# HGRN level operands copied aside for three tiled runs per unit, and a longer hold of whole-array products in the merge of threads

## The chip, the cores and the metric

One NeuronCore of a Trainium2 chip runs one launch of the kernel. The metric is device time in microseconds. The core has five engines with queues of their own: TensorE (PE; its weight loads are listed as PEld), VectorE (DVE), ScalarE (ACT), GpSimd (POOL) and SyncE (SP, which issues most DMAs).

## The reference, cut to what matters

The reference is one inference step of a two-layer trunk: layer 0 is a gated DeltaNet beside sliding-window attention, layer 1 is HGRN2. A prompt of 2048 positions and a sample group of 8 x 8 positions share all weights. After each mixer stands an output part (projection, layer norm, gate). The change touches the HGRN2 recurrence, for each of 8 heads with 128 x 128 state:

```python
fg = lb + (1.0 - lb) * jax.nn.sigmoid(zf)
logf = jnp.log(jnp.maximum(fg, F_FLOOR))
k = (1.0 - lb) * jax.nn.sigmoid(-zf)
...
# S_t = diag(f_t) S_{t-1} + k_t v_t^T,  o_t = S_t^T q_t / sqrt(dk)
dec = masked_exp(causal, G_c[:, :, :, None, :] - G_c[:, :, None, :, :])
a = jnp.einsum('nhid,nhijd,nhjd->nhij', q_c, dec, k_c)
o = jnp.einsum('nhid,nhde->nhie', q_c * jnp.exp(G_c), s) + jnp.einsum('nhij,nhje->nhie', a, v_c)
```

For one pair of positions j < i of a chunk the matrix `a` holds the sum over the 128 channels of q_i, k_j and the product of the decays f between them.

## The kernel before

**Work.** Time runs through four stages: layer 0's mixer, layer 0's output part (`dense_post`), the HGRN mixer (`dense_hgrn`), layer 1's output part. In each, one low-priority thread `dense` issues the big projections as split-precision products, three 128 x 128 matmuls per slice of the contraction (`product`). Its results go to many small threads: attention tiles, DeltaNet units, HGRN units. In the HGRN mixer the loop runs over halves of the prompt, heads and groups of 128-position chunks; each (head, group) is a unit (`hgrn_unit`). The groups have 4, 2, 2, 4 and 4 chunks, so there are 24 units of four chunks and 16 of two; for one group the 64 sample positions follow (`hgrn_sample`, 8 units). At most three units are in flight (`UNITS`), and each reserves memory before it starts: `7 * ... + RH` columns of an arena of 50 x 1024.

**HGRN core.** `hgrn_core` (L1716) builds `A`, the matrix `a` transposed, chunk by chunk, by doubling levels. Operands q and k are scaled in place on DVE so that, at level s, the k of the left half of each block of 2s positions and the q of the right half carry all decays between them. Then the products of that level are matmuls on TensorE with 32 columns of k as weights (`prod`), and their place in the 32 x 32 diagonal block is picked by a mask (`copy_predicated` on DVE). Levels 1 and 2 and the diagonal are made as elementwise products and summed over channels by matmuls with a matrix of ones (`sums`). Levels 32 and 64 go straight into `A` by ACT copies. As q and k are scaled in place, scaling to level 2s waits until TensorE has read level s. So a unit issues six separate runs of small matmuls: `sums`, 4, 8, 16, 32, 64.

**Tiled and whole.** A matmul whose weights have 32 or 64 rows or columns uses a part of the array ("tiled"); several of them run side by side. The rest are 128*128 ("whole"). In the profile the form of a weight load (128*32, 128*64, 32*32) tells which.

**Order of work.** All threads are Python generators; `run` (L525) is a list scheduler at build time that merges them into one fixed order for each engine. It keeps a model clock per engine, ranks the next instruction of each thread by when it could start, and emits the first. A TensorE instruction is ranked `MARGIN` (700 ns) after its operands are ready. The model counts 100 ns for a change from whole to tiled and 213 ns back (`SWITCH`), and these lines keep the rank free of the change itself but put whole products `STAY` later while the array stands tiled:

```python
s = self.start(o, MARGIN if o.eng == "tensor" else 0, True)
if o.eng == "tensor" and self.mode != o.mode:
    s -= SWITCH[o.mode == WHOLE] - STAY * (o.mode == WHOLE)
```

The order is fixed at build time; on the chip every engine works through its queue and waits on semaphores where an operand is late. All instructions are issued by one helper (line L354), so the profile's rows are told apart by tile names: `ar` is the arena, `bank` PSUM, `cst` the constants.

Of the kernel before, what the change touches and what calls it, by code (L numbers as in the profile page):

```python
# [46 lines left out]
FIRSTW, LASTG, WO0, WO1, GB = 30, 12, 6, 8, 2  # L47
PREP, WG0 = 2, 1
DMARGIN = 0
RD, RH = 8, 256  # L50
NBLK = 50
UNITS = (6, 5, 3)
XBUDGET = [18, 20]
# [524 lines left out]
class Step(Sched):  # L578
# [1134 lines left out]
        u["f"], u["k"] = e1, e2  # L1713
        self.dirty = True

    def hgrn_core(self, np_, n, cs, q, k, f, levels, out, own):  # L1716
# [33 lines left out]
        for s in levels + (2 * levels[-1],):  # L1750
            if s > 1:
                hs, nbk = s // 2, W // s
                qv = QF.rearrange("p (b r i) -> p b r i", r=2, i=hs)
                kv = k.rearrange("p (b r i) -> p b r i", r=2, i=hs)
                bv = B.rearrange("p (b r) -> p b r", r=2)
                yield self.V.tensor_tensor(out=qv[:, :, 1, :], in0=qv[:, :, 1, :], in1=bc(bv[:, :, 0], 2, hs), op=ALU.mult)
                yield self.V.tensor_tensor(out=kv[:, :, 0, :], in0=kv[:, :, 0, :], in1=bc(bv[:, :, 1], 2, hs), op=ALU.mult)
                if Bs is None:
                    Bs = yield al(W)
                B = Bs[:, bo : bo + nbk]  # L1760
                bo += nbk
                yield self.V.tensor_tensor(out=B, in0=bv[:, :, 0], in1=bv[:, :, 1], op=ALU.mult)
                if s == 2 and own:
                    self.free(f)
            if s > levels[-1]:
                break
            if s == 1:
                continue
            ps = yield bank()
            if s == 2:  # L1770
                Q4, K4, P4 = cut(QF, 4), cut(k, 4), kdb[:, :W].rearrange("p (b j i) -> p b j i", j=2, i=2)
                for j in range(2):
                    yield self.V.tensor_tensor(out=P4[:, :, j, :], in0=Q4[:, :, 2:4], in1=bc(K4[:, :, j], 2, 2), op=ALU.mult)
                yield from sums(ps, n * 48, Ab, 32)
                yield from sums(ps, 0, P1[:, : W // 2], 16)
                yield from sums(ps, n * 16, kdb[:, :W], 32)
                yield self.V.tensor_tensor(out=Dv, in0=cut(ps[:np_, n * 48 : n * 80], 32), in1=bc(self.c("ident32")[:np_], 1, n), op=ALU.mult)
                yield self.G.memset(ap=Ab[:np_], constant=0.0)
                D2, D4 = Dv.rearrange("p c (b i) -> p c b i", i=2), Dv.rearrange("p c (b i) -> p c b i", i=4)
                yield self.V.copy_predicated(out=D2[:, :, :, 1], mask=bc(cut(self.c("m1")[:np_], 2)[:, :, 1].bitcast(U32), 1, n), data=cut(ps[:np_, : n * 16], 16))  # L1780
                for j in range(2):
                    d = ps[:np_, n * 16 : n * 48].rearrange("p (c b j i) -> p c b j i", b=8, j=2, i=2)[:, :, :, j, :]
                    yield self.V.copy_predicated(out=D4[:, :, :, 2:4], mask=bc(cut(self.c(("m2", "m2o")[j])[:np_], 4)[:, :, 2:4].bitcast(U32), 1, n), data=d)
                self.free(P1)
            elif s <= 16:
                yield from prod(ps, QF)
                yield self.V.copy_predicated(out=Dv, mask=bc(self.c(f"m{s}")[:np_].bitcast(U32), 1, n), data=cut(ps[:np_, : n * 32], 32))
            else:

                cor = [(j, s) for j in range(0, 128, 2 * s)]  # L1790
                for c in range(n):
                    for j, _ in cor:
                        t = c * cs + j
                        yield self.P.matmul(out=ps[j : j + s, c * s : (c + 1) * s], lhsT=k[:, t : t + s], rhs=QF[:, t + s : t + 2 * s], start=True, stop=True)
                for j, _ in cor:
                    yield self.A.activation(out=A[j : j + s, :, j + s : j + 2 * s], in_=cut(ps[j : j + s, : n * s], s), func=AF.Copy)
# [12 lines left out]
    def hgrn_unit(self, half, h, hh, gi, u, vs):  # L1809
# [50 lines left out]
    def hgrn_sample(self, h, q, k, f, v, sg):  # L1860
# [4 lines left out]
        yield from self.hgrn_core(ST, 1, ST, q, k, f, (1, 2, 4), r, False)  # L1865
# [279 lines left out]
```

## Time and profile before

| | us |
|---|---|
| median of 3 runs | 3143.66 |
| lowest, highest | 3141.78, 3158.1 |
| profiled execution, its own time | 3148.57 |
| its span in the trace | 3146.8 |

| slice of the span | PE busy | DVE busy | ACT busy | granted PE clock |
|---|---|---|---|---|
| 0 to 400 us | 371.08 | 258.89 | 206.74 | 0.96 |
| 800 to 1200 us | 382.80 | 283.40 | 221.12 | 0.97 |
| 1200 to 1600 us | 395.36 | 163.98 | 55.43 | 1.00 |
| 2000 to 2400 us | 387.59 | 282.65 | 140.39 | 0.98 |

Each row of the second table is a stretch of 400 us; the columns are the time in which the engine executed something. A PE that is busy is not a PE at its peak: a weight load that cannot overlap, or a pause shorter than the matmul pipeline, hides in it. The profile's own mean for a matmul includes its passage through the array, so the pace is read from the distance between starts.

### The profile page before, as it was taken

To read this page: it belongs to the slowest core of one execution; us is meant where nothing else is said; L and a number is where in the kernel's file an instruction comes from. 1 tells how busy PE (TensorE), PEld (TensorE's weight loads), DVE (VectorE), ACT (ScalarE), POOL (GpSimd) and SP (SyncE) were. 2 spreads that over 40 slices of the span, in tenths; PEclk is the share of its full clock that TensorE was granted. 3 is DMA by queue.
4 is the path that set the end of the run, shared out by engine and by line. 5 is a ranking of instruction groups with operands and counts; after the bars stand their busy time and mean duration, and the time that the engine had idled before them with its cause. 6 is when DMAs were issued, how large, how long until landed. Compare 5 with 4: busy or idle time off the path is not lost.

```text
span 3146.8 us, 63372 instructions
## 1 busy us (share of the span) xinstructions
PE 3054.1 (97%) x25592; PEld 2507.9 (80%) x25592; DVE 1962.1 (62%) x5693; ACT 1149.5 (37%) x3074; POOL 197.1 (6%) x265
## 2 busy tenths in 40 slices
PE   8999899999999999999999999998999999999999
PEld 7787777877877787878888888786888888787787
DVE  5567776776757674333457686868577576733333
ACT  4455454655555561111143332324333333311011
POOL 0000000000000001111000000000000000111110
PEclk9999999999989999999999999999999999999999
DMA  4231222321214264233322122213111121732331
GB/s 118 70 86 41 59 69 61 95 63 47 81 48 121 77 174 107 75 82 89 104 74 69 42 69 67 65 56 99 56 52 52 46 69 49 221 87 75 82 86 49
DMA packets 320837, 246.45 MB, mean 78 GB/s; under 512 B 33800, under 2 KB 285840, under 8 KB 320528
## 3 DMA queue, kind: packets, MB, share of 16 engines
q1 hardware_dynamic: 253408, 207.80, 21.8%
q0 software_dynamic: 67136, 34.61, 6.1%
q8 instruction: 201, 3.29, 0.4%
q14 instruction: 92, 0.75, 0.1%
HBM read 182.98 MB, written 60.45 MB: 77 GB/s over the span
## 4 chain that ended last, share of the span: by engine, by line
PE 57%; DVE 7%; DMA 4%; issue 3%; ACT 2%; POOL 0%; SPq 0%; POOLq 0%; DVEq 0%; ACTq 0%
PE bank L354 57%; DVE ar L354 7%; DMA ar<-in_w_in_odd 2%; ACT ar L354 2%; DMA ar<-in_w_in_even 1%; POOL ar L354 0%; SPq L354 0%; DMA ar<-gd 0%; DMA ar<-in_w_ple_gate 0%; DMA ar<-x 0%; DMA os<-ar 0%; ACT L354 0%; DMA ar<-in_w_out_even 0%; DMA ctail<-ar 0%; DMA gd<-ar 0%
## 5 line engine op out<-in xcount | busy, mean ns | idle before, releaser
L354 PE MATMUL bank<-ar,ar 128*128 128x512 f32 (+10 forms) x20168 | 2865.9, 306 | 55.5 <-DVE ar L354 30.8
L354 PEld LDWEIGHTS bank<-ar,ar 128*128 128x128 f32 (+4 forms) x20168 | 2250.9, 163 | 490.4 <-issue 85.8
L354 ACT ACTIVATE ar<-bank 128x128 f32<-128x128 f32 (+13 forms) x1471 | 528.0, 369 | 1343.8 <-PE bank L354 1250.5
L354 DVE TENSOR_TENSOR ar<-ar,ar 128x256 f32<-128x256 f32 (+9 forms) x1517 | 737.1, 514 | 245.2 <-ACT ar L354 207.5
L354 ACT ACTIVATE ar<-ar 128x1024 fp32r<-128x1024 f32 (+12 forms) x833 | 443.1, 551 | 581.7 <-DMA ar<-in_pT 248.6
L354 DVE SCALAR_TENSOR_TENSOR ar<-ar,bank 128x512 f32<-128x512 f32 (+3 forms) x256 | 164.1, 641 | 393.4 <-ACT ar L354 261.6
L354 PE MATMUL bank<-cst,ar 128*128 128x128 f32 (+4 forms) x1439 | 244.2, 280 | 21.1 <-DVE ar L354 14.7
L354 PEld LDWEIGHTS bank<-cst,ar 128*128 128x128 f32 (+4 forms) x1439 | 172.9, 141 | 72.4 <-issue 19.0
L354 DVE TENSOR_TENSOR ar<-bank,ar 128x128 fp32r<-128x128 f32 (+7 forms) x326 | 147.6, 455 | 80.7 <-ACT ar L354 45.2
L354 POOL TENSOR_TENSOR ar<-ar,mhalf 128x2 f32<-128x2 f32 (+3 forms) x104 | 107.6, 1035 | 1361.6 <-DVE ar L354 978.5
L354 DVE TENSOR_TENSOR ar<-ar 128x256 f32<-128x256 f32 (+11 forms) x575 | 135.6, 248 | 15.4 <-ACT ar L354 14.1
L354 DVE SCALAR_TENSOR_TENSOR ar<-bank,ar,ar 128x509 f32<-128x509 f32 (+8 forms) x216 | 123.0, 573 | 26.2 <-ACT ar L354 24.7
L354 DVE COPY_PREDICATED ar<-cst,bank 128x128 f32<-128x128 uint32 (+4 forms) x356 | 93.0, 262 | 72.7 <-PE bank L354 61.5
L354 PEld LDWEIGHTS bank<-ar 128*32 128x32 f32 (+4 forms) x2904 | 90.5, 121 | 45.5 <-DVE ar L354 17.9
L354 PE MATMUL bank<-ar 128*32 128x32 f32 (+5 forms) x2904 | 116.8, 212 | 8.2 <-DVE ar L354 6.9
L354 DVE SCALAR_TENSOR_TENSOR ar<-ar,ar,bank 128x128 f32<-128x128 f32 x192 | 65.7, 342 | 74.1 <-PE bank L354 72.6
L354 POOL MEMSET ar<- 128x256 f32 (+4 forms) x85 | 29.0, 348 | 1141.7 <-PE bank L354 772.8
L354 DVE SCALAR_TENSOR_TENSOR ar<-ar,ar,ar 128x1024 f32<-128x1024 f32 (+1 forms) x68 | 87.0, 1279 | 13.4 <-POOL ar L354 13.3
L354 POOL DMA_DIRECT2D ar<-os x64 | 57.4, 898 | 283.1 <-PE bank L354 214.1
L354 DVE SCALAR_TENSOR_TENSOR ar<-ar,ar 128x512 f32<-128x512 f32 (+10 forms) x187 | 55.9, 304 | 30.4 <-ACT ar L354 29.1
L354 DVE TENSOR_SCALAR ar<-bank 128x512 f32<-128x512 f32 (+2 forms) x80 | 44.6, 592 | 36.2 <-ACT ar L354 35.8
L354 ACT ACTIVATION_READ_ACCUMULATOR ar<-bank 128x1 f32 (+1 forms) x340 | 66.4, 195 | 0.2
(55 smaller groups left out, 820.7 us busy)
## 6 DMA issues: line engine op xcount, KB each, us to landing
ar<-os POOLq DMA_DIRECT2D x64, 512.0 KB, 4.9
ar<-in_w_in_odd SPq DMA_DIRECT2D x64, 512.0 KB
ar<-in_w_in_even SPq DMA_DIRECT2D x60, 512.0 KB
os<-ar SPq DMA_DIRECT2D x36, 512.0 KB
ar<-x SPq DMA_DIRECT2D x32, 512.0 KB
os<-ar SPq DMA_DIRECT2D x56, 256.0 KB
ar<-in_x_prompt SPq DMA_DIRECT2D x16, 512.0 KB
ar<-in_w_ple_gate SPq DMA_DIRECT2D x16, 512.0 KB
```

What stands on the lines that cost most here:

```text
L354: o.fn = lambda: f(**kw)
```

## The change

`hgrn_core` gets a flag `deep` (true for the prompt, false for the samples) in place of the list of levels. For the prompt, ACT copies the scaled k and the right halves of q of level 4 into `KA`, `QA` and those of level 8 into `KB`, `QB`, so that DVE can go on scaling in place; then levels 4, 8 and 16 are multiplied in one run into one bank, with 16 moved columns in place of 32. In the same way the operands of level 32 are copied to `KC`, `QC`, and levels 32 and 64 share a run and a bank. A unit has three runs. `level` copies 16 columns per chunk where 32 were copied. For the samples, level 4 follows `sums` in the same run. The reserve per unit grows (`RH`), and `STAY` goes from 40 to 1000 ns.

```diff
-RD, RH = 8, 256
+RD, RH = 8, 512
...
-STAY = 40
+STAY = 1000
...
+        def scale(s):
+            nonlocal B, Bs, bo
+            hs, nbk = s // 2, W // s
+            qv = QF.rearrange("p (b r i) -> p b r i", r=2, i=hs)
+            kv = k.rearrange("p (b r i) -> p b r i", r=2, i=hs)
+            bv = B.rearrange("p (b r) -> p b r", r=2)
+            yield self.V.tensor_tensor(out=qv[:, :, 1, :], in0=qv[:, :, 1, :], in1=bc(bv[:, :, 0], 2, hs), op=ALU.mult)
+            yield self.V.tensor_tensor(out=kv[:, :, 0, :], in0=kv[:, :, 0, :], in1=bc(bv[:, :, 1], 2, hs), op=ALU.mult)
...
-        def prod(ps, qq):
+        def prod(ps, c0, kk, qq):
             for c in range(n):
                 for r in range(nb):
-                    t = slice(c * cs + 32 * r, c * cs + 32 * r + 32)
-                    yield self.P.matmul(out=ps[rows[r], c * 32 : c * 32 + 32], lhsT=k[:, t], rhs=qq[:, t], start=True, stop=True)
+                    t = c * cs + 32 * r
+                    yield self.P.matmul(out=ps[rows[r], c0 + c * 16 : c0 + c * 16 + 16], lhsT=kk[:, t : t + 32], rhs=qq(c * nb + r), start=True, stop=True)
...
+        def level(ps, c0, s):
+            d = Dv.rearrange("p c (b r i) -> p c b r i", r=2, i=s)[:, :, :, 1, :]
+            m = self.c(f"m{s}")[:np_].rearrange("p (b r i) -> p b r i", r=2, i=s)[:, :, 1, :]
+            x = ps[:np_, c0 : c0 + n * 16].rearrange("p (c b i) -> p c b i", c=n, i=s)
+            yield self.V.copy_predicated(out=d, mask=bc(m.bitcast(U32), 1, n), data=x)
...
-            elif s <= 16:
-                yield from prod(ps, QF)
-                yield self.V.copy_predicated(out=Dv, mask=bc(self.c(f"m{s}")[:np_].bitcast(U32), 1, n), data=cut(ps[:np_, : n * 32], 32))
...
+            KA, QA = kdb, P1
+            ops = []
+            for s, kk, qq in ((4, KA, QA), (8, KB, QB)):
+                yield self.A.activation(out=kk[:, :W], in_=k, func=AF.Copy)
+                yield self.A.activation(out=cut(qq[:, : W // 2], s), in_=right(QF, s), func=AF.Copy)
+                ops.append((kk, cut(qq[:, : W // 2], 16)))
+                yield from scale(2 * s)
             ps = yield bank()
...
+            for i, (kk, qq) in enumerate(ops):
+                yield from prod(ps, i * n * 16, kk, lambda b: qq[:, b])
+            q16 = right(QF, 16)
+            yield from prod(ps, 2 * n * 16, k, lambda b: q16[:, b])
+            self.free(P1, QB)
+            yield from scale(32)
+            KC, QC = (cut(KB[:, i * W // 2 : (i + 1) * W // 2], 32) for i in range(2))
+            yield self.A.activation(out=KC, in_=k.rearrange("p (b r i) -> p b r i", r=2, i=32)[:, :, 0, :], func=AF.Copy)
+            yield self.A.activation(out=QC, in_=right(QF, 32), func=AF.Copy)
+            for i, s in enumerate((4, 8, 16)):
+                yield from level(ps, i * n * 16, s)
             self.freebank(ps)
+            yield from scale(64)
+            ps = yield bank()
+            for c in range(n):
+                for b in range(2):
+                    yield self.P.matmul(out=ps[64 * b : 64 * b + 32, c * 32 : (c + 1) * 32], lhsT=KC[:, 2 * c + b], rhs=QC[:, 2 * c + b], start=True, stop=True)
+            for c in range(n):
+                t = c * cs
+                yield self.P.matmul(out=ps[0:64, n * 32 + c * 64 : n * 32 + (c + 1) * 64], lhsT=k[:, t : t + 64], rhs=QF[:, t + 64 : t + 128], start=True, stop=True)
...
-        yield from self.hgrn_core(128, nt, 128, q[:, :Wp], k[:, :Wp], f[:, :Wp], SMALL + (32, 64), r, not smp)
+        yield from self.hgrn_core(128, nt, 128, q[:, :Wp], k[:, :Wp], f[:, :Wp], True, r, not smp)
```

More of the change, by code (lines that the diff above doesn't have):

```diff
@@ L1714, in gates, with hgrn_core @@
         self.dirty = True
-    def hgrn_core(self, np_, n, cs, q, k, f, levels, out, own):
+    def hgrn_core(self, np_, n, cs, q, k, f, deep, out, own):
         W = n * cs
@@ L1728, in hgrn_core, with right @@
         B = f
-        def prod(ps, qq):
+        def scale(s):
[6 more added lines that the diff above has]
+            yield self.V.tensor_tensor(out=kv[:, :, 0, :], in0=kv[:, :, 0, :], in1=bc(bv[:, :, 1], 2, hs), op=ALU.mult)
+            if Bs is None:
+                Bs = yield al(W)
+            B = Bs[:, bo : bo + nbk]
+            bo += nbk
+            yield self.V.tensor_tensor(out=B, in0=bv[:, :, 0], in1=bv[:, :, 1], op=ALU.mult)
+        def prod(ps, c0, kk, qq):
             for c in range(n):
                 for r in range(nb):
-                    t = slice(c * cs + 32 * r, c * cs + 32 * r + 32)
-                    yield self.P.matmul(out=ps[rows[r], c * 32 : c * 32 + 32], lhsT=k[:, t], rhs=qq[:, t], start=True, stop=True)
+                    t = c * cs + 32 * r
+                    yield self.P.matmul(out=ps[rows[r], c0 + c * 16 : c0 + c * 16 + 16], lhsT=kk[:, t : t + 32], rhs=qq(c * nb + r), start=True, stop=True)
+        def right(x, s):
+            return x.rearrange("p (b r i) -> p b r i", r=2, i=s)[:, :, 1, :]
+        def level(ps, c0, s):
[3 more added lines that the diff above has]
+            yield self.V.copy_predicated(out=d, mask=bc(m.bitcast(U32), 1, n), data=x)
         def sums(ps, c0, x, w):
@@ L1749, in hgrn_core @@
         yield self.V.tensor_tensor(out=P1[:, : W // 2], in0=Q2[:, :, 1], in1=K2[:, :, 0], op=ALU.mult)
[L1750 to L1768, printed above, removed]
-            ps = yield bank()
[L1770 to L1784, printed above, removed]
-            elif s <= 16:
-                yield from prod(ps, QF)
-                yield self.V.copy_predicated(out=Dv, mask=bc(self.c(f"m{s}")[:np_].bitcast(U32), 1, n), data=cut(ps[:np_, : n * 32], 32))
[L1788 to L1796, printed above, removed]
-            self.freebank(ps)
@@ new lines, in hgrn_core @@
+        yield from scale(2)
+        if own:
+            self.free(f)
+        Q4, K4, P4 = cut(QF, 4), cut(k, 4), kdb[:, :W].rearrange("p (b j i) -> p b j i", j=2, i=2)
+        for j in range(2):
+            yield self.V.tensor_tensor(out=P4[:, :, j, :], in0=Q4[:, :, 2:4], in1=bc(K4[:, :, j], 2, 2), op=ALU.mult)
+        if deep:
+            KB = yield al(W)
+            QB = yield al(W // 2)
+        else:
+            yield from scale(4)
+        ps = yield bank()
+        yield from sums(ps, n * 48, Ab, 32)
@@ new lines, in hgrn_core @@
+        yield from sums(ps, 0, P1[:, : W // 2], 16)
+        yield from sums(ps, n * 16, kdb[:, :W], 32)
+        if deep:
+            yield from scale(4)
+        else:
+            q4 = QF.rearrange("p (g b r i) -> p g b r i", b=4, r=2, i=4)[:, :, :, 1, :]
+            yield from prod(ps, n * 80, k, lambda b: q4[:, b])
+        yield self.V.tensor_tensor(out=Dv, in0=cut(ps[:np_, n * 48 : n * 80], 32), in1=bc(self.c("ident32")[:np_], 1, n), op=ALU.mult)
+        yield self.G.memset(ap=Ab[:np_], constant=0.0)
@@ new lines, in hgrn_core @@
+        D2, D4 = Dv.rearrange("p c (b i) -> p c b i", i=2), Dv.rearrange("p c (b i) -> p c b i", i=4)
+        yield self.V.copy_predicated(out=D2[:, :, :, 1], mask=bc(cut(self.c("m1")[:np_], 2)[:, :, 1].bitcast(U32), 1, n), data=cut(ps[:np_, : n * 16], 16))
+        for j in range(2):
+            d = ps[:np_, n * 16 : n * 48].rearrange("p (c b j i) -> p c b j i", b=8, j=2, i=2)[:, :, :, j, :]
+            yield self.V.copy_predicated(out=D4[:, :, :, 2:4], mask=bc(cut(self.c(("m2", "m2o")[j])[:np_], 4)[:, :, 2:4].bitcast(U32), 1, n), data=d)
@@ new lines, in hgrn_core @@
+        if not deep:
+            yield from level(ps, n * 80, 4)
+            yield from scale(8)
+        self.freebank(ps)
+        if deep:
+            KA, QA = kdb, P1
[5 more added lines that the diff above has]
+                yield from scale(2 * s)
+            ps = yield bank()
+            for i, (kk, qq) in enumerate(ops):
[9 more added lines that the diff above has]
+                yield from level(ps, i * n * 16, s)
+            self.freebank(ps)
+            yield from scale(64)
+            ps = yield bank()
+            for c in range(n):
[4 more added lines that the diff above has]
+                yield self.P.matmul(out=ps[0:64, n * 32 + c * 64 : n * 32 + (c + 1) * 64], lhsT=k[:, t : t + 64], rhs=QF[:, t + 64 : t + 128], start=True, stop=True)
+            self.free(KB)
+            yield from scale(128)
+            for j in (0, 64):
+                yield self.A.activation(out=A[j : j + 32, :, j + 32 : j + 64], in_=cut(ps[j : j + 32, : n * 32], 32), func=AF.Copy)
+            yield self.A.activation(out=A[0:64, :, 64:128], in_=cut(ps[0:64, n * 32 : n * 96], 64), func=AF.Copy)
+            self.freebank(ps)
+        else:
+            self.free(P1)
@@ L1864, in hgrn_sample @@
         yield self.Q.dma_start(out=S, in_=self.a["state_hgrn_c"][:, h].rearrange("b k v -> k b v"))
-        yield from self.hgrn_core(ST, 1, ST, q, k, f, (1, 2, 4), r, False)
+        yield from self.hgrn_core(ST, 1, ST, q, k, f, False, r, False)
         zz = yield from self.spread(r["qd"][:, 0, :])
```

## The prediction

> **What bounds the kernel now.** First the page: span, busy shares, the chain that ended last.
>
> ```profile
> span 3146.8 us, 63372 instructions
> PE 3054.1 (97%) x25592; PEld 2507.9 (80%) x25592; DVE 1962.1 (62%) x5693; ACT 1149.5 (37%) x3074; POOL 197.1 (6%) x265
> ...
> PE 57%; DVE 7%; DMA 4%; issue 3%; ACT 2%; POOL 0%; SPq 0%; POOLq 0%; DVEq 0%; ACTq 0%
> ```
>
> TensorE is busy 97% of the span and leads the chain. The next view cuts the span into the four stages (even-layer mixer, its output part, HGRN mixer, its output part): length, then busy time of PE, PEld, DVE, ACT, POOL, then granted clock, DMA share, GB/s.
>
> ```profile
> 0.00:1200.00 1200.00, 1143.67 (x11046) 931.60 (x11047) 828.39 (x2721) 649.04 (x1811) 37.95 (x69) 0.97 0.30 82
> 1200.00:1600.00 400.00, 395.36 (x1820) 320.75 (x1819) 163.98 (x272) 55.43 (x114) 43.68 (x41) 1.00 0.36 93
> 1600.00:2860.00 1260.00, 1233.75 (x11451) 1029.46 (x11450) 862.97 (x2537) 415.43 (x1095) 83.94 (x126) 0.99 0.25 71
> 2860.00:3147.00 287.00, 281.35 (x1281) 226.05 (x1279) 106.74 (x164) 29.56 (x55) 31.56 (x29) 0.99 0.29 72
> ```
>
> In the HGRN stage PE lacks 1260 - 1233.75 = 26 us of being always busy; DVE is at 68%, ACT at 33%. So what counts is how much time the order of work takes on PE. The two output stages have almost no tiled matmuls; the change acts on the first and the third. Now the timeline of weight loads (PEld) through one HGRN unit of four chunks: start, busy time, form, count, idle before and what ended it.
>
> ```profile
> 2006.52 0.35 PEld L354 LDWEIGHTS bank<-ar 128*32 128x32 f32 x32 [0.19 <-DVE ar L354]
> 2006.91 1.76 PEld L354 LDWEIGHTS bank<-ar,ar 128*128 128x128 f32 x12
> 2008.86 0.35 PEld L354 LDWEIGHTS bank<-ar 128*32 128x32 f32 x32 [0.19 <-issue]
> 2009.25 1.76 PEld L354 LDWEIGHTS bank<-ar,ar 128*128 128x128 f32 x12
> 2011.20 0.35 PEld L354 LDWEIGHTS bank<-ar 128*32 128x32 f32 x32 [0.19 <-issue]
> 2011.59 2.20 PEld L354 LDWEIGHTS bank<-ar,ar 128*128 128x128 f32 x15
> 2013.98 0.33 PEld L354 LDWEIGHTS bank<-ar 128*32 128x32 f32 x16 [0.19 <-DVE ar L354]
> 2014.36 1.91 PEld L354 LDWEIGHTS bank<-ar,ar 128*128 128x128 f32 x13
> 2016.46 0.54 PEld L354 LDWEIGHTS bank<-ar 128*64 128x64 f32 x8 [0.19 <-DVE ar L354]
> 2017.07 1.18 PEld L354 LDWEIGHTS bank<-ar,ar 128*128 128x128 f32 x8
> 2018.44 0.27 PEld L354 LDWEIGHTS bank<-ar,cst 128*32 128x32 f32 x16 [0.19 <-issue]
> 2018.75 0.42 PEld L354 LDWEIGHTS bank<-cst,ar 128*128 128x128 f32 x4
> 2019.14 0.19 PEld L354 LDWEIGHTS bank<-ar,ar 128*128 128x128 f32 x1
> 2019.48 0.16 PEld L354 LDWEIGHTS bank<-ar,cst 128*32 128x32 f32 x8 [0.16 <-issue]
> 2019.73 0.54 PEld L354 LDWEIGHTS bank<-ar,ar 128*128 128x128 f32 x4
> ```
>
> The three rows of 32 are levels 4, 8 and 16 (16 fp32 matmuls, two loads each), the 16 is level 32, the 8 is level 64; the last two tiled rows are the next unit's `sums`, split in two. Between them stand whole-array products. Each tiled run has a fixed price: from 2008.86 to 2009.25 it holds the loads for 0.39, plus 0.19 idle before, 0.58 us for 32 loads; the run of 8 costs 0.25 + 0.16 = 0.41. The 24 loads between them cost 0.17, 0.007 each, which leaves 0.41 - 0.06 = 0.35 fixed. The 8 are wider (64 columns), so I take **0.33 us per run**; bounds 0.19 (only the idle ahead) and 0.41 (all of the short run).
>
> **The change, part by part.** From the code there are 40 units (8 heads, 5 groups of tiles): 24 of four chunks, 16 of two. Savings are negative, in us.
>
> 1. Levels 4, 8, 16 go in one run in place of three: 40 x 2 x 0.33 = **-26.4** (-15.2 to -32.8). It is PE time in the stage where PE is the bound, so it goes off the end.
>
> 2. Their moved operands shrink from 32 to 16 columns; the count stays. Within the runs the 32 loads take 0.35, the last one about 0.11 itself, so (0.35 - 0.11)/31 = 7.7 ns a load at 32 columns; the 16 `sums` loads (half 64, half 32 columns, mean 48) take (0.27 - 0.11)/15 = 10.7. That slope of 0.19 ns a column would give 4.7 ns at 16 columns: 3 ns x (24 x 96 + 16 x 48 = 3072 loads) = 9. No run here is so narrow and a floor may come first, so I take **-4** (0 to -9).
> The Trainium skill, TensorEngine Tiling (Array Packing), Performance Considerations, speaks against this step: "A matmul with free_dim=1 has same latency as free_dim=60." By that rule this term is 0 and the sum 4 us higher; the trace's difference between 32 and 48 columns speaks mildly against the rule, though it is not at one width each.
>
> 3. Levels 32 and 64 share a bank and a run, but of two shapes (128*32, then 128*64). Bounds: nothing saved if the change of shape costs what a change to whole arrays does, 0.33 if none. The trace has one place where such runs touch, with no idle between, at half clock (0.50 in its window):
>
> ```profile
> 2198.08 0.19 PEld L354 LDWEIGHTS bank<-ar,cst 128*32 128x32 f32 x4 [0.65 <-DVE ar L354]
> 2198.33 0.50 PEld L354 LDWEIGHTS bank<-ar,ar 128*64 128x64 f32 x4
> ```
>
> ```profile
> 2191.00:2208.10 17.10, 11.13 (x104) 7.93 (x103) 13.73 (x56) 6.15 (x19) 0.39 (x2) 0.50 0.39 112
> ```
>
> I take 0.15: 40 x 0.15 = **-6** (0 to -13). In the 8 sample units level 4 joins the `sums`: 8 x 0.33 = **-2.6** (0 to -3.3).
>
> 4. Six ACT copies per unit are new: operands of levels 4 and 8, then of 32. Rows of the HGRN stage, by shape:
>
> ```profile
> L354 ACT ACTIVATE ar<-ar 128x512 f32<-128x512 f32 x48 | 29.0, 629 | 1.8 <-DVE ar L354 1.4
> L354 ACT ACTIVATE ar<-ar 128x256 f32<-128x256 f32 x16 | 6.3, 415 | 3.3 <-DVE ar L354 3.3
> L354 DVE COPY_PREDICATED ar<-cst,bank 128x128 f32<-128x128 uint32 x72 | 21.6, 300 | 29.3 <-PE bank L354 28.2
> L354 DVE COPY_PREDICATED ar<-cst,bank 128x64 f32<-128x64 uint32 x120 | 32.5, 271 | 13.4 <-PE bank L354 10.6
> ```
>
> Four chunks: 2 x 0.629 + 4 x 0.415 = 2.9 us; two chunks: 2 x 0.415 + 4 x 0.30 (extrapolated) = 2.0. Together 24 x 2.9 + 16 x 2.0 = 102 us of ACT, 33% to 41% of the stage, beside PE. The 72 predicated copies, halved, go from 300 to about 271 ns: 2 us of DVE, also beside PE. The new wait is DVE's: the in-place scaling to 8, to 16 and to 64 must not start before ACT has read. Behind it in DVE's queue stand the other units' gate arithmetic and bank evacuations, which free the three banks of the dense products. The chain itself hardly grows: a level now takes 2.34 us (2008.86 to 2011.20); afterwards scaling (about 1.0 us) plus copies (0.629 + 0.415) and two hand-overs, about 2.3. Cover is the 700 ns by which the merge ranks a tiled matmul after its operands. If it is gone PE waits; I put **+4** (0 to +15).
> The pool is 256 columns larger for each of at most three units, 768 of 51200. No wait for memory shows in the 26 us of idle PE: 0, at most some of the +15. DMA issues stay as they are; SP's queue is passed by nothing.
>
> 5. STAY from 40 to 1000: while the array is tiled, whole products rank 1 us later, so a tiled run due within about a microsecond joins the one before. Counted in the timeline, whole-array stretches between two tiled runs (start to start) shorter than 0.5 us are 92: 50 in the first stage, 42 in HGRN; from 0.5 to 1.05 us 95 more. First and last of the 187 (the stretch and the tiled run that ends it):
>
> ```profile
> 55.59 0.19 PEld L354 LDWEIGHTS bank<-ar,ar 128*128 128x128 f32 x1 [0.38 <-issue]
> 55.96 0.20 PEld L354 LDWEIGHTS bank<-ar,ar 128*64 128x64 f32 x4 [0.19 <-issue]
> ...
> 2692.08 0.76 PEld L354 LDWEIGHTS bank<-ar,ar 128*128 128x128 f32 x4
> 2692.96 0.16 PEld L354 LDWEIGHTS bank<-ar,cst 128*32 128x32 f32 x8
> ```
>
> In 52 of the 92 both runs have one shape (0.33 each), in 40 two shapes (0.15): 23 us. The 95 are a toss: their operands come at about the time when the run would start, and what isn't saved is waited. 46 of the 50 in HGRN are the split `sums`, where the second product is still on DVE. I take half of the 23: **-12** (-30 to +35; the bad end is priced below).
>
> Sum: -26.4 - 4 - 6 - 2.6 + 4 - 12 = -47. The profiled execution took 3148.57 us, so 3101.6; the median of the runs is 0.16% below it, which would give 3097. I forecast **3099 us**, 1.4% faster than 3143.66. About 0.5% (16 us) can be told from no change.
>
> **The rivals.**
>
> *The hold does nothing (0.16).* Within one unit the next tiled run often waits for an ACT or DVE step; with the 0.7 us added it ranks beyond the hold. If the near ones too are bound by other things, only -35 is left: 3113. Against it: the 92 short stretches.
>
> *The hold leaves PE waiting (0.10), slower.* One mechanism: PE stands in tiled shape for a run whose operand is late on DVE or ACT, with whole products queued behind. With 187 held runs and a mean saving of (124 x 0.33 + 63 x 0.15)/187 = 0.27 us, a mean wait w costs 187 x (w - 0.27). The rest of the change saves 35, so the kernel is slower by 0.5% from w = 0.27 + 51/187 = 0.54 us; at 0.6 it is +62 - 35, 3176 us. For it, the waits of PEld (total, times, longest), on DVE in the HGRN stage:
>
> ```profile
> PEld bank L354 <- DVE ar L354: 51.6, 112, 2.4
> ```
>
> and on ACT in the first stage:
>
> ```profile
> PEld bank L354 <- ACT ar L354: 57.5, 104, 7.7
> ```
>
> These are 0.46 and 0.55 us a time, with 0.19 of the plain passage in each, although the merge leaves 0.7 us. Against it: those are the late ones alone; most runs wait 0.19.
>
> *The clock (0.08).* Full runs of tiled matmuls are followed by half clock. The timeline of weight loads, then windows around its end (granted clock third from the right):
>
> ```profile
> 142.62 3.87 PEld L354 LDWEIGHTS bank<-ar,ar 64*64 64x64 f32 x49 [0.19 <-issue]
> ```
>
> ```profile
> 143.00:146.40 3.40, 3.40 (x47) 3.15 (x46) 0.00 (x0) 0.00 (x0) 0.00 (x0) 1.00 0.00 0
> 146.40:153.20 6.80, 6.80 (x45) 5.96 (x44) 0.82 (x4) 1.22 (x4) 0.00 (x0) 0.50 0.00 0
> ```
>
> Longer tiled stretches could bring more. If the granted clock went from 0.97 to 0.95 in the first stage (24 us) and 0.99 to 0.975 in the third (19), +43 - 47: 3144. Against it: most tiled runs last 0.4 us beside microseconds of whole products.
> The Trainium skill, TensorE: Matmul & The Clock Gate, Why this matters for your kernels, asks only for no PE-idle gaps over about 3 us; by that rule waits below 1 us cost no clock and this rival falls. The rows above disagree: PE shows busy all of 143.0 to 146.4, and the clock halves.
>
> *More than forecast (0.10).* Run prices at their upper bound and all 92 merged: about -75, 3073.
>
> **How the numbers follow.** The forecast (3080 to 3125) has 0.56. Range: 3070 takes in most of the fifth case; 3140 the hold that does nothing, part of the clock and a hold that eats half of the gain; outside stay the slower rival, half of the clock's and a tail below. Faster by over 0.5% (below 3128): 0.54 of the forecast, 0.13 of the hold without effect, 0.10, 0.01: 0.78. Within 0.5%: 0.02 + 0.03 + 0.04 + 0.05 = 0.14. Slower: 0.06 + 0.02 = 0.08.
>
> **What would show it.** Right: in HGRN one 128*32 run of 96 loads (four chunks) of about 1.0 us where three of 0.58 were, then one run of 128*32 and 128*64; third stage shorter by about 37 us, first by about 7. Part 2 is right if a load takes about 6 ns there. Part 5 is right if stretches below 0.5 us are nearly gone and PEld's waits have not grown; wrong if waits on DVE and ACT grow by more than 20 us. The forecast fails if the third stage gains under 20 us: then PE was not its bound, or ACT's copies make DVE, and then PE, wait.

## The result, and the profile after

| us | before | after |
|---|---|---|
| median of 5 runs each, taken together | 3147.03 | 3127.15 |
| lowest, highest | 3141.78, 3158.1 | 3119.46, 3131.65 |
| profiled execution, its own time | 3148.57 | 3119.46 |

The ratio is 0.9931 with a 95% interval of 0.9908 to 0.9954: faster by 0.69%, 20 us where the forecast had 1.4%. The profiled execution of the changed kernel is the lowest of its five runs, so the two profiles differ by more (29 us) than the medians do.

The page of the changed kernel, its span and its busy times:

```profile
span 3117.7 us, 63598 instructions
PE 3002.6 (96%) x25592; PEld 2498.8 (80%) x25592; DVE 1964.8 (63%) x5693; ACT 1228.3 (39%) x3314; POOL 198.7 (6%) x265
```

The count of matmuls is the same. PE is busy for 52 us less, but the span is only 29 us shorter: PE now waits more. ACT has 240 instructions more (6 in each of 40 units) and 79 us more work.

To compare equal work, both traces are cut at the same two stores (the last of layer 0's result, and that of the sample output), into layer 0, the HGRN part, and the rest. The windows, first of the changed kernel, then of before; columns as in the prediction (length, PE, PEld, DVE, ACT, POOL, clock, DMA share, GB/s):

```profile
0.00:1597.10 1597.10, 1524.66 (x12856) 1249.36 (x12856) 991.85 (x2977) 701.60 (x1917) 82.24 (x110) 0.98 0.31 84
1597.10:2922.30 1325.20, 1287.96 (x11874) 1092.57 (x11874) 901.51 (x2608) 507.04 (x1362) 97.38 (x138) 0.99 0.26 74
2922.30:3117.70 195.40, 189.94 (x865) 156.92 (x863) 71.43 (x109) 19.68 (x36) 19.12 (x17) 0.99 0.30 74
```

```profile
0.00:1593.60 1593.60, 1537.11 (x12856) 1250.62 (x12856) 987.37 (x2977) 701.38 (x1917) 81.64 (x110) 0.98 0.31 84
1593.60:2951.40 1357.80, 1327.07 (x11875) 1100.32 (x11874) 903.19 (x2609) 428.38 (x1122) 96.39 (x138) 0.99 0.25 72
2951.40:3146.80 195.40, 189.94 (x865) 156.92 (x863) 71.53 (x109) 19.70 (x36) 19.11 (x17) 0.99 0.30 75
```

The HGRN part is 32.6 us shorter. Layer 0, which of the change gets only the hold, is 3.5 us longer although PE is busy there for 12.5 us less: its idle time went from 56.5 to 72.4. The last part is equal.

The timeline of weight loads through one HGRN unit of four chunks, after (start, busy time, form, count, idle before and what ended it):

```profile
1997.33 0.64 PEld L354 LDWEIGHTS bank<-ar,ar 128*32 128x32 f32 x64 [0.19 <-ACT ar L354]
1998.06 0.35 PEld L354 LDWEIGHTS bank<-ar 128*32 128x32 f32 x32
1998.43 2.35 PEld L354 LDWEIGHTS bank<-ar,ar 128*128 128x128 f32 x16
2000.97 0.33 PEld L354 LDWEIGHTS bank<-ar 128*32 128x32 f32 x16 [0.19 <-issue]
2001.87 0.54 PEld L354 LDWEIGHTS bank<-ar 128*64 128x64 f32 x8 [0.56 <-DVE ar L354]
2002.47 0.59 PEld L354 LDWEIGHTS bank<-ar,ar 128*128 128x128 f32 x4
```

```profile
2147.70 0.27 PEld L354 LDWEIGHTS bank<-ar,cst 128*32 128x32 f32 x16 [0.19 <-ACT ar L354]
2148.78 0.16 PEld L354 LDWEIGHTS bank<-ar,cst 128*32 128x32 f32 x8 [0.81 <-DVE ar L354]
2149.03 0.63 PEld L354 LDWEIGHTS bank<-ar,ar 128*128 128x128 f32 x5
```

The 64 and 32 loads are levels 4, 8 and 16 in one run, as forecast. The next run begins with level 32 and then stands for 0.56 us in tiled shape until DVE has scaled for level 64. In the second fence `sums` is one run and no longer two, but with a wait of 0.81 us inside it: the whole products that used to stand in that gap are held back.

What PEld waits for in layer 0 (total us, times, longest), after and before:

```profile
PEld bank L354 <- ACT ar L354: 68.4, 100, 7.3
PEld bank L354 <- issue: 65.9, 191, 3.5
PEld bank L354 <- DVE ar L354: 52.6, 88, 2.8
```

```profile
PEld bank L354 <- issue: 80.4, 221, 5.0
PEld bank L354 <- ACT ar L354: 58.1, 105, 7.7
PEld bank L354 <- DVE ar L354: 43.8, 76, 2.5
```

Less is lost on changes of shape ("issue", 30 fewer), more on operands: 10.3 us more on ACT, 8.8 more on DVE. The same view of the HGRN part, after and then before (where the row on DVE is the 51.6 us that the prediction quotes):

```profile
PEld bank L354 <- DVE ar L354: 38.0, 76, 2.1
PEld bank L354 <- issue: 34.0, 108, 1.9
PEld bank L354 <- ACT ar L354: 21.8, 39, 2.3
```

```profile
PEld bank L354 <- issue: 47.2, 141, 1.1
PEld bank L354 <- ACT ar L354: 4.9, 8, 1.4
```

These rows put an idle time down to the last releaser, and PE counts as busy through short pauses, so they don't add up to the change. A fuller account comes from the starts of all matmuls in the trace: each distance from one start to the next is booked to one cause. "Pace" is the distance that the shape has when nothing stands in the way (for whole products the median of the shape; for tiled ones up to 0.13 us, so that a change between two tiled shapes is in it). Entering a run costs up to 0.1 us beyond the pace. Leaving it costs the whole distance to the first whole product, and the product after that another 0.03 to 0.13. Everything longer is a wait. Two things are rough in this: any other whole product that is 0.03 to 0.13 us late is booked under leaving too (28 to 34 us in HGRN and 40 to 44 in layer 0, whatever the kernel), and whole products that start sooner than the median are not set off, so that a column adds up to 14 to 25 us more than its part took. So only differences between kernels are read from it; they agree with the differences in length to 2 us. Sums in us:

| | layer 0 before | layer 0 after | HGRN before | HGRN after |
|---|---|---|---|---|
| tiled runs | 362 | 278 | 337 | 146 |
| whole products at pace | 1207.5 | 1207.5 | 1067.9 | 1067.7 |
| tiled ones at pace | 128.9 | 141.2 | 103.6 | 120.7 |
| entering and leaving runs | 168.5 | 137.0 | 145.1 | 81.3 |
| waits ahead of a run | 35.2 | 23.2 | 17.9 | 4.4 |
| **waits inside runs** | 30.6 | **61.1** | 26.1 | **51.8** |
| waits between whole products | 46.8 | 51.9 | 11.5 | 14.8 |

In both parts PE saves on entering and leaving and waits more, inside runs above all. In HGRN the saving is the larger: -46.7 with the pace, against +15.5 for the three kinds of wait. In layer 0 it isn't: -19.2 against +23.6.

### The profile page after: what moved, and what is told of

The parts are those of the page before. It is cut to its first block, busy times and chain, and to the rows that moved or that the text cites. A ratio compares the mean times of both kernels' runs of the same rounds, so it can differ in the third digit from the quotient of the medians.

```text
span 3117.7 us, 63598 instructions
## 1 busy us (share of the span) xinstructions
PE 3002.6 (96%) x25592; PEld 2498.8 (80%) x25592; DVE 1964.8 (63%) x5693; ACT 1228.3 (39%) x3314; POOL 198.7 (6%) x265
## 5 line engine op out<-in xcount | busy, mean ns | idle before, releaser
L354 PE MATMUL bank<-ar,ar 128*128 128x512 f32 (+10 forms) x20432 | 2813.2, 302 | 67.2 <-ACT ar L354 39.8
L354 DVE TENSOR_TENSOR ar<-ar,ar 128x256 f32<-128x256 f32 (+8 forms) x1500 | 732.6, 517 | 247.9 <-ACT ar L354 210.3
L354 ACT ACTIVATE ar<-ar 128x512 f32<-128x512 f32 (+15 forms) x1067 | 527.8, 522 | 750.0 <-DVE ar L354 384.6
L354 PE MATMUL bank<-cst,ar 128*128 128x128 f32 (+3 forms) x1439 | 239.7, 279 | 27.5 <-DVE ar L354 16.4
L354 PEld LDWEIGHTS bank<-cst,ar 128*128 128x128 f32 (+3 forms) x1439 | 173.5, 141 | 73.8 <-DVE ar L354 16.9
L354 DVE TENSOR_TENSOR ar<-ar 128x4 f32<-128x4 f32 (+10 forms) x592 | 139.9, 250 | 19.9 <-ACT ar L354 13.3
L354 PEld LDWEIGHTS bank<-ar 32*32 32x32 f32 (+3 forms) x2640 | 88.8, 121 | 38.9 <-ACT ar L354 13.6
L354 PE MATMUL bank<-ar 32*32 32x32 f32 (+5 forms) x2640 | 113.7, 209 | 4.5 <-ACT ar L354 2.3
L354 DVE COPY_PREDICATED ar<-cst,bank 128x64 f32<-128x64 uint32 (+3 forms) x356 | 85.9, 242 | 34.9 <-PE bank L354 24.4
L354 POOL MEMSET ar<- 128x256 f32 (+4 forms) x85 | 29.1, 348 | 961.1 <-PE bank L354 550.6
L354 DVE SCALAR_TENSOR_TENSOR ar<-ar,ar 128x4 f32<-128x4 f32 (+10 forms) x190 | 58.4, 312 | 31.7 <-ACT ar L354 30.5
```

Source lines behind the costliest of these rows:

```text
L354: o.fn = lambda: f(**kw)
```

## The experiments

All ratios are against the kernel before, run on the same chip in the same turn. "Layer 0" and "HGRN" are the lengths of the first two windows, cut at the same stores.

**1. The new HGRN core with the old hold.** The question is what the rebuilt levels are worth alone.

```diff
-STAY = 1000
+STAY = 40
```

> The changed HGRN core with the old hold (STAY 40). Theory A (the hold pays back in waits what it saves in drains; the HGRN rebuild carries the gain): 3110 to 3125 us, that is 22 to 37 below before (3147) and not slower than the changed kernel (3127); the first stage ends about 4 us earlier than in the changed kernel. Theory B (the hold is worth the 12 us of the forecast and the HGRN rebuild fell short): about 3139 us, 12 slower than the changed kernel.

Measured: 3134.33 us, ratio 0.9961 (0.9949 to 0.9974), between the two theories; HGRN 1344.0 us. So the rebuild alone brings 0.39%, not the 35 us of the prediction's sum without part 5. The timeline of weight loads in one unit of this kernel says why:

```profile
2004.25 0.85 PEld L354 LDWEIGHTS bank<-ar,ar 128*32 128x32 f32 x65 [0.19 <-ACT ar L354]
2005.41 2.72 PEld L354 LDWEIGHTS bank<-ar,ar 128*32 128x32 f32 x48 [0.31 <-DVE ar L354]
2008.72 0.33 PEld L354 LDWEIGHTS bank<-ar 128*32 128x32 f32 x16 [0.58 <-ACT ar L354]
2009.09 0.30 PEld L354 LDWEIGHTS bank<-ar,ar 128*128 128x128 f32 x2
2009.71 2.37 PEld L354 LDWEIGHTS bank<-ar,ar 128*64 128x64 f32 x20 [0.32 <-DVE ar L354]
```

The view joins a whole product to its neighbour where the names are the same: 65 is 64 tiled loads and one whole, 48 is 32 tiled and 16 whole, 20 is 8 tiled and 12 whole. Levels 4 and 8 go together, then one whole product, then level 16; level 32, two loads of whole products, then level 64. The three runs of the code are five. Over the whole HGRN part there are 266 runs, where the changed kernel has 146: **with this order of products the three runs per unit come from the hold, not from the code.**

**2. The old HGRN core with the new hold.**

```diff
-STAY = 40
+STAY = 1000
```

> The kernel before with the long hold alone (STAY 1000). Theory A: 3140 to 3160 us, no gain: fewer tiled runs in both mixer stages, but PE stands inside them as long as was saved; the first stage 4 us longer than before. Theory B: about 3135 us, 12 below before.

Measured: 3162.33 us, ratio 1.0050 (1.0037 to 1.0063), slower, just beyond Theory A. Layer 0 took 1603.7 us, HGRN 1365.0. PEld's waits on DVE in its HGRN part, where before had 51.6:

```profile
PEld bank L354 <- DVE ar L354: 65.2, 129, 2.0
```

The hold alone costs time in both parts, though it took 80 runs out of HGRN (254 for 337) and 84 out of layer 0. So it isn't a gain added to another: it helps only where the new core gives it something to hold together.

**3. The new core with a hold of 400 ns.**

```diff
-STAY = 1000
+STAY = 400
```

> The changed kernel with a hold of 400 ns, which is shorter than the 700 ns that a tiled matmul's rank has in hand, so that a run joins the one before only if its operand should already be there. Theory A: drains saved without most of the waits, 3100 to 3118 us, the fastest of the four. Theory B: between the hold of 40 and that of 1000, 3127 to 3139 us.

Measured: 3125.52 us, ratio 0.9942 (0.9926 to 0.9957); layer 0 1600.3 us, HGRN 1335.5 with 219 runs. HGRN lies between the holds of 40 (1344.0) and 1000 (1325.2), so it wants the long hold. The total is that of the changed kernel within the intervals, and between the ranges of the two theories.

**4. The hold of 1000 in HGRN only.**

```diff
-STAY = 1000
+STAY = (40, 1000)
...
-                    s -= SWITCH[o.mode == WHOLE] - STAY * (o.mode == WHOLE)
+                    s -= SWITCH[o.mode == WHOLE] - STAY[self.late] * (o.mode == WHOLE)
```

`self.late` becomes 1 where `dense_hgrn` starts.

> The changed kernel with STAY 40 in layer 0 and 1000 from the HGRN mixer on. Theory A with the loss of the hold in the first stage alone: first stage as before (4 us earlier than changed), rest as changed, 3120 to 3125 us. Theory B: the hold gains in the first stage too, 3130 to 3135 us.

Measured: 3115.45 us, ratio 0.9903 (0.9889 to 0.9917). Its windows:

```profile
0.00:1593.50 1593.50, 1535.21 (x12856) 1248.29 (x12856) 987.55 (x2977) 701.60 (x1917) 81.76 (x110) 0.98 0.31 84
1593.50:2918.70 1325.20, 1288.55 (x11874) 1093.38 (x11874) 901.51 (x2608) 507.41 (x1362) 97.27 (x138) 0.99 0.26 74
```

HGRN is the same 1325.2 us as in the changed kernel, and layer 0 is back at its old length. The ratio is better by 0.0028, some 9 us; the intervals of the two just overlap. It is 5 us below Theory A's range. The profiles point the same way, though their ranges touch: layer 0 without the hold took 1588.2 to 1597.3 us in nine profiles (mean 1591.5), with the hold of 1000 it took 1597.1 and 1603.7.

**5. Latest operand first, with the hold in HGRN.** If a run falls apart because its first product is ready before its last, then issuing the product first whose operand comes last should keep it whole with no hold at all. Here the order is turned round in all three runs, on top of experiment 4.

```diff
-        yield from sums(ps, n * 48, Ab, 32)
-        yield from sums(ps, 0, P1[:, : W // 2], 16)
         yield from sums(ps, n * 16, kdb[:, :W], 32)
+        yield from sums(ps, 0, P1[:, : W // 2], 16)
+        yield from sums(ps, n * 48, Ab, 32)
...
-            for i, (kk, qq) in enumerate(ops):
-                yield from prod(ps, i * n * 16, kk, lambda b: qq[:, b])
             q16 = right(QF, 16)
             yield from prod(ps, 2 * n * 16, k, lambda b: q16[:, b])
+            for i, (kk, qq) in reversed(list(enumerate(ops))):
+                yield from prod(ps, i * n * 16, kk, lambda b: qq[:, b])
```

In the same way level 64 goes ahead of level 32, and level 4 of the samples ahead of `sums`.

> As e4 (hold of 1000 in HGRN only), and within each tiled run of a unit the product whose operand comes last is issued first: level 16 before 8 and 4, level 64 before 32, the sums of levels 2, 1, diagonal in this order. Theory A (inside its runs PE waits for the operand that DVE finishes last): 3100 to 3109 us against 3115 of e4, with the waits inside tiled runs of the HGRN stage falling by 8 us or more. Theory B (what is waited inside a run is waited ahead of it instead): 3112 to 3119 us.

Measured: 3116.02 us, ratio 0.9896 (0.9877 to 0.9916); HGRN 1321.2 us with 135 runs. With the hold in place the order adds little: 4 us in the profile, nothing in the medians. This is Theory B: by the account of starts the waits inside runs fell from 52.2 us in experiment 4 to 37.4, but those ahead of runs and between whole products rose, and the sum is 70.1 in both.

**6. Latest operand first, no hold.**

```diff
-STAY = (40, 1000)
+STAY = (40, 40)
```

> As e5 with the old hold of 40 everywhere. Theory A (without the hold the runs of a unit fall apart because their first product is ready before their last; this order keeps them whole by itself): 3105 to 3117 us against 3134 of e1, and about as few tiled runs in the HGRN stage as with the long hold. Theory B (the long hold is needed, or it joins runs of different threads that matter): 3125 to 3134 us.

Measured: 3114.02 us, ratio 0.9885 (0.9866 to 0.9903), the lowest ratio of all here, and in Theory A's range. Experiment 1 has the same hold and the same products in the old order, and stood at 0.9961 (0.9949 to 0.9974): **the order alone is worth 0.76%.** HGRN has 148 runs, as many as with the long hold. One unit in the timeline of weight loads, and the window of the HGRN part:

```profile
1999.87 0.54 PEld L355 LDWEIGHTS bank<-ar,ar 128*64 128x64 f32 x8 [0.20 <-DVE ar L355]
2000.48 0.33 PEld L355 LDWEIGHTS bank<-ar 128*32 128x32 f32 x16
2000.86 2.28 PEld L355 LDWEIGHTS bank<-ar,ar 128*128 128x128 f32 x17
2003.08 0.46 PEld L355 LDWEIGHTS bank<-cst,ar 128*128 128x128 f32 x4
2003.81 0.33 PEld L355 LDWEIGHTS bank<-ar,cst 128*32 128x32 f32 x24 [0.26 <-DVE ar L355]
```

```profile
1597.30:2919.80 1322.50, 1283.08 (x11875) 1090.37 (x11875) 903.18 (x2609) 510.79 (x1362) 96.59 (x138) 0.98 0.26 74
```

Levels 64 and 32 follow each other with no wait between (0.56 us in the changed kernel), and the 24 loads of `sums` are one group (0.81 us of wait in their midst there). But by the account of starts the waits inside runs (29.1 us for 51.8) only moved: ahead of runs they are 17.5 (4.4), between whole products 23.5 (14.8), together 70.1 for 71.0. So HGRN is about as long as with the hold (1322.5 and 1325.2 us); what the order brings is that it needs none.

**7. Are 16 moved columns cheaper than 32?** On top of experiment 4 each product of levels 4, 8 and 16 moves its 16 columns twice, side by side; only the first half is read.

```diff
+                    if deep:
+                        o = 2 * c0 + c * 32
+                        yield self.P.matmul(out=cut(ps[rows[r], o : o + 32], 16), lhsT=kk[:, t : t + 32], rhs=bc(qq(c * nb + r), 1, 2), start=True, stop=True)
+                        continue
                     yield self.P.matmul(out=ps[rows[r], c0 + c * 16 : c0 + c * 16 + 16], lhsT=kk[:, t : t + 32], rhs=qq(c * nb + r), start=True, stop=True)
...
```

> As e4, with 32 moved columns in levels 4, 8 and 16 (the same 16 twice; the second half of the output is not read). If 16 columns are no cheaper than 32, as the 8.5 ns a load of the changed kernel's run of 96 suggests: 3111 to 3119 us, as e4. If the 3 ns a load of the forecast's upper bound were there: about 3124 us.

Measured: 3114.01 us, ratio 0.9896 (0.9879 to 0.9912), against 0.9903 (0.9889 to 0.9917) of experiment 4: no cost. The loads of levels 4, 8 and 16 in one unit:

```profile
1989.09 0.65 PEld L355 LDWEIGHTS bank<-ar,ar 128*32 128x32 f32 x64 [0.19 <-ACT ar L355]
1989.82 0.35 PEld L355 LDWEIGHTS bank<-ar 128*32 128x32 f32 x32
1990.21 2.35 PEld L355 LDWEIGHTS bank<-ar,ar 128*128 128x128 f32 x16
```

From first load to first whole product are 1.12 us; the changed kernel, with 16 columns, took 1.10 (1997.33 to 1998.43). Over the 23 such runs the medians, from the last whole start before to the first after and less the pace, are 1.08 and 1.05 us. By the working of the prediction a load takes (0.65 - 0.11)/63 = 8.6 ns here and (0.64 - 0.11)/63 = 8.4 there.

**8. Every ACT copy twice**, on top of experiment 4.

```diff
+                for _ in range(2):
-                yield self.A.activation(out=kk[:, :W], in_=k, func=AF.Copy)
-                yield self.A.activation(out=cut(qq[:, : W // 2], s), in_=right(QF, s), func=AF.Copy)
+                    yield self.A.activation(out=kk[:, :W], in_=k, func=AF.Copy)
+                    yield self.A.activation(out=cut(qq[:, : W // 2], s), in_=right(QF, s), func=AF.Copy)
```

`KC` and `QC` likewise.

> As e4, with each of the six ACT copies of a prompt unit issued twice, 102 us more of ACT in the HGRN stage. If ACT's copies lie beside PE but for the 4 us of the forecast: 3115 to 3121 us. If they stand in the chain that PE waits for: 3130 us or more.

Measured: 3130.83 us, ratio 0.9946 (0.9930 to 0.9963), 0.0043 above experiment 4, or 13.5 us. The window of its HGRN part, and PEld's longest wait there:

```profile
1588.20:2927.30 1339.10, 1287.58 (x11874) 1095.13 (x11873) 906.28 (x2608) 581.36 (x1602) 98.19 (x138) 0.98 0.26 73
```

```profile
PEld bank L355 <- DMA ar<-os: 10.5, 2, 9.2
```

HGRN is 13.9 us longer with PE as busy as before (1287.58 for 1288.55). Of that 10.5 us stand in this row, most of it in one wait of 9.2 us. It ends at 2667.8 us, where the HGRN units run out (the last tiled run starts at 2679): the output part waits for a load of `os`, where the units store their results, and PE's order has nothing else at that place. Experiment 4 has no wait above 2.5 us after the first 10 us of this part. So ACT's copies aren't free beside PE, but this price hangs on one place in the order. It is that of a second set; the first was not measured by itself.

**9 and 10. Does layer 0 gain from a hold of 400 ns?** On top of experiment 6, in layer 0 only, then everywhere.

```diff
-STAY = (40, 40)
+STAY = (400, 40)
```

> As e6 (latest operand first), with a hold of 400 ns in layer 0 and 40 in the HGRN stage. Theory A (a hold costs where it joins runs whose operands are not there; 400 lies within the 700 ns in hand): 8 to 10 us below e6, 3104 to 3110, with the waits inside tiled runs of the first stage growing by less than 8 us. Theory B (any hold in layer 0 is paid back): 3114 to 3120 us.

Measured: 3118.24 us, ratio 0.9911 (0.9894 to 0.9928), Theory B. With (400, 400):

> As e9 with the hold of 400 in the HGRN stage too. Theory A: as e9 or up to 6 us below it (few runs are left to join). Theory B: 3114 us or more.

Measured: 3121.08 us, ratio 0.9905 (0.9886 to 0.9924), Theory B again. Neither is better than no hold (0.9885, 0.9866 to 0.9903). In experiment 9 layer 0 has 318 runs for 362, and entering and leaving cost 151.8 us for 168.5 in the kernel before. But the waits between whole products rose from 46.8 to 56.9 (those above 0.5 us from 25.0 to 38.9), where the nine profiles with the hold of 40 in layer 0 have 41 to 51: part of the time saved on the change of shape comes back as waiting. The 4 us that the account leaves as a gain lie within the scatter of layer 0's length in those nine.

**11. Level 32 in a run of its own,** on top of experiment 6: straight from `k` and `QF`, into its own bank, without `KC`, `QC` and their copies.

```diff
-            KC, QC = (...)
-            yield self.A.activation(out=KC, ...)
-            yield self.A.activation(out=QC, ...)
+            p32 = yield bank()
+            for c in range(n):
+                for j in range(2):
+                    t = c * cs + 64 * j
+                    yield self.P.matmul(out=p32[64 * j : 64 * j + 32, c * 32 : (c + 1) * 32], lhsT=k[:, t : t + 32], rhs=QF[:, t + 32 : t + 64], start=True, stop=True)
```

> As e6, but level 32 is multiplied in a run of its own from the operands in place, as in the kernel before, without its two ACT copies. If the join of 32 and 64 brings what the run lengths show (0.57 and 0.80 us apart, 1.18 together, 0.19 a unit, 8 us): 3120 to 3124 us. If the copies' place in the chain eats it: 3110 to 3116 us.

Measured: 3117.98 us, ratio 0.9905 (0.9887 to 0.9924). That is 0.002, or 6 us, above experiment 6, and 4 us by the medians, with intervals that overlap, and between the two ranges: inconclusive, at most a small gain for the join.

**12. The kernel before, with the order of `sums` alone turned round:** level 2, level 1, diagonal.

```diff
-                yield from sums(ps, n * 48, Ab, 32)
-                yield from sums(ps, 0, P1[:, : W // 2], 16)
                 yield from sums(ps, n * 16, kdb[:, :W], 32)
+                yield from sums(ps, 0, P1[:, : W // 2], 16)
+                yield from sums(ps, n * 48, Ab, 32)
```

> The kernel before with one edit: the sums of a unit issue the product whose operand comes last first (level 2, level 1, diagonal). Theory A (46 split sums cost about 0.23 us each: 0.67 and 0.44 apart, 0.88 whole): 8 to 10 us below before. Theory B (the split was filled with useful whole products): within 3 us of before.

Measured: 3133.30 us, ratio 0.9956 (0.9939 to 0.9973); HGRN 1349.3 us with 283 runs for 337. In the profile HGRN is 8.5 us shorter, as Theory A had it; the ratio says 14, with an interval of 8 to 19. Two moved lines, with no new instruction and no hold, give as much as the whole rebuild without the hold (0.9961).

**The account of the HGRN part in all of these**, by starts of matmuls as above, in us; the middle column is entering, leaving and tiled ones at pace, the next the three kinds of wait together:

| kernel | runs | entering, leaving, pace | waits | length |
|---|---|---|---|---|
| before | 337 | 248.7 | 55.5 | 1357.8 |
| 12: before, `sums` turned | 283 | 239.3 | 56.7 | 1349.3 |
| 2: before, hold 1000 | 254 | 241.8 | 70.1 | 1365.0 |
| 1: new core, hold 40 | 266 | 225.6 | 66.0 | 1344.0 |
| 3: new core, hold 400 | 219 | 221.5 | 61.8 | 1335.5 |
| after: new core, hold 1000 | 146 | 202.0 | 71.0 | 1325.2 |
| 6: new core, turned, hold 40 | 148 | 201.0 | 70.1 | 1322.5 |
| 11: as 6, level 32 apart | 195 | 210.5 | 69.6 | 1332.5 |
| 8: hold 1000, copies twice | 136 | 203.7 | 83.5 | 1339.1 |

Every kernel waits 4.3 to 5.5 us for the load of `x` where layer 0 ends. In experiment 1 this wait starts just behind the cut and in the other rows just ahead of it, so its 4.3 us are left out of that row.

The new core waits more than the old one whatever the hold: 66 us with the old hold for 55.5, 10.5 more; 62 with the hold of 400; 70 to 71 with the long hold and with the order turned (experiments 5 and 6). But the old core with the long hold waits 70.1 too. So with the old hold some 10 us come with the rebuilt levels, and the table can't divide the rest between levels, hold and order. What the hold and the order change most is the cost of entering and leaving: 225.6 us for 202.0 and 201.0.

## Why the prediction was right in sign and too large

The time, 3127 us, lies in the range of 3070 to 3140, and the sign and the stage were right. The gain was less than half of the forecast. By the prediction's steps:

**Part 5, the hold (-12), is the step that failed.** Its premise was that a run held together saves 0.33 us and waits little. In layer 0 it saved 19.2 us over 84 runs, 0.23 each, and waited 23.6 us, 0.28 each. That is the mechanism of the rival "the hold leaves PE waiting", at its break-even of 0.27 and not at the 0.6 that the rival was priced with. The waits inside runs are the sure part: 61.1 us here and 60.0 in experiment 2, against 30.3 to 31.6 in the nine profiles of layer 0 with the hold of 40. The net cost of 4 us is less than the 9 us by which the lengths of those nine differ. The rows show such a run in layer 0 of the changed kernel, by the timeline of weight loads:

```profile
281.22 0.32 PEld L354 LDWEIGHTS bank<-ar,ar 32*32 32x32 f32 x8 [0.35 <-issue]
283.15 1.35 PEld L354 LDWEIGHTS bank<-ar,ar 32*32 32x32 f32 x13 [1.60 <-ACT ar L354]
```

PE stands in tiled shape for 1.60 us until ACT delivers. The short stretches did vanish: below 0.5 us one is left in layer 0 and three in HGRN, of 92. The prediction's own sign of failure, waits of PEld on DVE and ACT up by more than 20 us, came: +19.1 in layer 0 and +3.3 in HGRN. Experiments 2 and 4 show the cost by itself: +0.50% with the old core, and about 9 us in layer 0, where the intervals of the two ratios just overlap. In HGRN with the new core the hold did gain, 18.8 us (1344.0 to 1325.2), more than part 5 gave it there (5.5, for 42 of the 92 stretches); but that gain is what parts 1 and 3 had already booked.

**Parts 1 and 3 were right in price and wrong in what makes them happen.** The prediction took "three runs" from the code and booked -35 for it without the hold. Experiment 1 gives 10 us by the medians (14 in HGRN by the profile) for that: the merge puts whole products into gaps between an early operand and a late one, so the runs fall apart. With the hold (4) or with the order turned round (6) they stay whole, and then HGRN comes near the forecast: it was to be 37 us shorter (the terms themselves add up to 40.5 there) and is 32.6 shorter in the changed kernel. Of that nearness a part is luck. The savings came to 46.7 us where parts 1, 2, 3 and the share of 5 had 44.5, although part 2 gave nothing, because 191 runs went and the parts count 149; and the waits took 15.5 where part 4 had 4. So the rival "the hold does nothing" (3113) rested on the same error: without the hold most of parts 1 and 3 goes too. The price of a run: from the last whole start before it to the second after, less the pace, three runs of 32 loads take 3 x 0.58 = 1.75 us and the one of 96 takes 1.15 (medians), so 0.30 per run saved where I took 0.33. The join of 32 and 64 saves 0.18 where nothing waits inside (experiment 6: 0.20 + 0.99 us, against 0.38 + 0.61 + 2 x 0.19 = 1.37 apart; I took 0.15), but nothing in the changed kernel's unit above: 0.19 + 1.50, because level 64 is 0.56 us late.

**Part 2 (-4) was nothing.** Experiment 7 prices 16 and 32 columns alike, 8.4 and 8.6 ns a load. The slope that I drew came from two kinds of runs, of 32 and of 48 columns on the mean, and does not go on below 32; whether the columns make it at all, no run tested. The Trainium skill's rule, quoted in the prediction from TensorEngine Tiling (Array Packing), Performance Considerations, gave 0 here, and the runs agree.

**Part 4 (+4) was too small: about +10 with the old hold, +15 in the changed kernel.** The table shows it, 66.0 us of waits with the hold of 40 and 71.0 with that of 1000, against 55.5; the part's bounds ended at +15. The amount of work was right. The ACT rows of the HGRN stage, after:

```profile
L354 ACT ACTIVATE ar<-ar 128x512 f32<-128x512 f32 x96 | 59.4, 628 | 74.3 <-DVE ar L354 74.1
L354 ACT ACTIVATE ar<-ar 128x256 f32<-128x256 f32 x144 | 55.7, 408 | 62.5 <-DVE ar L354 52.4 <-PE bank L354 9.9
L354 ACT ACTIVATE ar<-ar 128x128 f32<-128x128 f32 x64 | 17.5, 298 | 18.7 <-DVE ar L354 16.0 <-PE bank L354 2.7
```

Against the 29.0 and 6.3 us that the prediction quotes (the third shape is new) they are 97 us more, where 102 were estimated; the engine's total rose by 79. What was mis-sized is how much of it lies beside PE. A second set of copies adds 13.4 us of waits again (83.5 for the 70.1 of experiment 4), most of it in the one wait of 9.2 us. Whether the first 10 to 15 us come from the copies, or from operands that now all have to be there for one run, isn't settled: no run left the whole first set out with the runs kept whole. Experiment 11 leaves out two of the six, and its waits are those of experiment 6 (69.6 and 70.1). PEld's waits on ACT in HGRN do rise with the new core, from 4.9 us to 21.8 (17.5 in experiment 1); with the order turned (6) they are 9.5 and those on DVE 53.2, so which engine is waited for follows the order.

**The other rivals.** The clock: the granted clock was at half speed for 106 us of the first two parts before and for 102 after, so longer runs brought no more of it. All 14 profiles have 96 to 130 us there; the rival's 43 us would have needed some 86 us more. More than forecast (-75): pace, entering and leaving gave -46.7 in HGRN and -19.2 in layer 0, together near that case, and waits of 39.1 took more than half of it back.

**Slips in the working of the prediction.** The times of the rivals are counted from the profiled execution (3148.57 us), some 5 us above the scale of the medians that the forecast stands on. And of the 50 stretches of 0.5 to 1.05 us in HGRN 37, not 46, stand between two parts of `sums` (11 more are shorter). The run ahead of the half clock, which the view prints by the form of its first load (64*64), is for the most part of 128*64 loads. None of this changes the account.

## What to carry to other kernels

- Where a list scheduler merges threads, a burst of small matmuls stays together of itself where its first is ready no sooner than its last: issue the product with the latest operand first. This gave 0.76% with the new core and 0.44% with the old one, for no instruction.
- A penalty that holds other work back to keep a burst whole trades a known drain for an unknown wait. Set the number of runs saved against the waits inside runs, in each stage by itself; here it paid in one stage, with one core, and not in the other.
- A busy engine does not show this trade: PE's busy time fell by 52 us and the span by 29. Read the distances between starts.

## What the runs showed of the hardware that I had not expected

- In runs of 128*32 matmuls the width of the moved operand does not show between 16 and 32 columns: 8.4 and 8.6 ns a load.
- A change between two tiled shapes isn't free: the join of levels 64 and 32 saved 0.18 us of the 0.30 that a run costs (experiment 6, where nothing waits inside).
- Layer 0 in the same order took 1588.2 to 1597.3 us in nine profiles, and the time at half clock in it was 61 to 89 us, most in the longest. So a single profile says nothing of a few us in layer 0.
- The order turned round moves the waits of the HGRN part and does not shorten them: 70.1 us in all with the hold (5) and without it (6), for 70.1 in experiment 4, while those inside runs are 37.4, 29.1 and 52.2. I have no explanation that a run tested.
